# Holding back two heads' convolution chains, taking an output product two k-tiles at a time over both units, and two changes of order, in a two-layer mLSTM and attention trunk

## The chip, the cores and the metric

The program runs on one core of one Trainium2 chip. A core has engines that run side by side, each with its own queue of instructions taken in order: TensorE (PE: matmuls; its weight loads are shown apart as PEld), VectorE (DVE), ScalarE (ACT), GpSimd (POOL) and SyncE (SP, which here issues the loads from memory). They wait for each other through semaphores. PE writes to PSUM, eight banks of 128 x 512 numbers; everything else lies in SBUF. The metric is the device time of one execution in microseconds (us), lower is better.

## The reference

256 tokens of width 1024 pass through two layers. Each layer is a half-step SwiGLU (width 2752), a mixing block, a second half-step SwiGLU and a gated addition of a per-layer input ("ple"). The mixing block is where the change works:

```python
u = rmsnorm(h, mix_norm)
z = u @ w_in
...
m_qk = jax.nn.silu(causal_dwconv(m_qk, m_conv_w, m_conv_b))
...
hm = mlstm_chunkwise(mq, mk, mv, ig, lf)
hm = head_rmsnorm(hm, m_out_norm.reshape(M_HEADS, M_HEAD_DIM)).reshape(bsz, t, M_WIDTH)
hm = (jax.nn.sigmoid(m_o.astype(jnp.float32)) * hm).astype(h.dtype)
...
ha = swa_gqa_sinks(aq, ak, av, a_sinks)

merged = jax.nn.sigmoid(g_m) * (hm @ w_branch_m) + jax.nn.sigmoid(g_a) * (ha @ w_branch_a)
h = h + merged @ w_out
```

`mlstm_chunkwise` is a matrix memory with 4 heads of 256, its queries and keys passed through a causal convolution of 4 taps and SiLU; `swa_gqa_sinks` is attention over a window of 128 tokens with 16 query heads of 64 and 4 key heads. All is float32.

## The kernel before

**Products in three parts.** A float32 number x is split into a high part (x cast to the matmul's type) and a low part (x minus the high part). A product is three matmuls: high x high, high x low, low x high. Weights come from memory by SP's loads into two raw buffers, 1 MB each. ScalarE casts the high part (`wh`), VectorE subtracts to get the low part (`wl`), 128 x 1024 at a time, called a part (two k-tiles of 512 columns). A ring of eight parts holds them; a part's place is free again when PE has used it (`drop`, line 400). Activations are split in the same way: `uT` (normed input), `hmT` (memory's output), `haT` = `qT` (attention), `mT` (merged), each with a high and a low tile, both transposed (features on partitions).

**Stages of the mixing block**, in the order in which PE runs them: keys and queries (`kvq`), values (`v`), gate A (`gt`), the input and forget gates (`if`), the memory's queries and keys of heads 0 and 1 (`z`, two jobs: part 0 queries, part 1 keys), attention's output product (`ya`), output gate (`og`), `z` of heads 2 and 3, gate M (`gt`), the memory's output product (`ym`), and the product with `w_out` (`yo`). Between them stand short pieces: attention's scores (`sc`, lines 1361 to 1407), its output (`ha`), the memory's scores (`st`), decay matrices (`wt`), outputs (`num`) and transposes (`tp`).

**The order is a planner's.** For PE, ScalarE, VectorE and SP the order of instructions on the chip is that in which the program emits them. Work beside the matmuls is written as generators, called chains; each `yield` marks a point at which the chain waits for an engine. `Clock` (line 63) keeps a planned time for each engine; every emitted instruction is charged a cost:

```python
 68    COST = {"tensor": (0.0, 1 / 2400), "scalar": (0.12, 1 / 1120), "vector": (0.12, 1 / 960), "gpsimd": (0.3, 0.17)}
 69    SYNC = 0.1
```

that is, a fixed part and a part per element of a row, in us; `SYNC` is added before another engine may use the result. `now` is PE's planned time. `tick` (line 201) goes through the list `bg` of chains in the order in which they were started and advances each one whose planned due time has come; then `feed` (line 336) may start the split of one more weight part. It does so if a place in the ring is free, the load has arrived by plan, and neither ScalarE nor VectorE is planned to be busy for longer than a slack from now, 3 us, or 2 us with four or more unused parts in store (line 343). A chain that PE needs at once is carried to its end by `finish` (line 226), which lets the planned time pass. `start` adds a chain and advances it once; `defer` adds one that runs at the next tick.

**Loops that matter here.** `project_halves` (line 475) makes products with features on the PSUM partitions, 256 tokens as columns. `units` are halves of the output, 512 features each; each unit has four parts (k-tiles 0-1, 2-3, 4-5, 6-7). The first two parts of all units run first (`todo[0]`), then the last two parts of the first unit, then of the second (`todo[1]`). A tick stands ahead of every six matmuls of 256 columns. When a unit has had its last part, `use` is called for each of its two pairs of k-tiles. For `ym` this is `use_m` (line 982): VectorE multiplies with gate M and adds gate A's share (two operations on `mg`), ScalarE casts the high half of `mT`, VectorE makes its low half. `project` (line 411) makes `yo` with tokens on the partitions and 512 columns; for each part and block of 128 tokens it ticks, waits by plan for `mT` of that k-tile (`xT.wait`), and emits the three matmuls, in which the low half of `mT` is wanted in the third.

The memory's output for head 3 is k-tiles 6 and 7 of `hmT`, the last ones written. `conv` (line 1158) takes one PSUM bank of `z`: ScalarE starts the sum, VectorE adds three taps for each of two k-tiles (six operations on `cv`), ScalarE applies SiLU, and the result is split into `qk`. `head` then makes the memory's scores from the query and key parts.

`norm` (line 639) prepares the next block's input. Between the layers (`between`) its transposed halves are put off until the ple product has been made (`crossed`), and then `to_T` (line 521) transposes and splits at once.

Of the kernel before, what the change touches and what calls it, by code (L numbers as in the profile page):

```python
# [19 lines left out]
P = 128  # L20
# [14 lines left out]
RING = 8  # L35
STORE, HASTE = 4, 3
AHEAD = (3.0, 2.0)
ACTIVE = 5
LAG = 1.5
WARM = 5  # L40
# [126 lines left out]
class Trunk:  # L167
# [7 lines left out]
    def __init__(self, ctx, tc, a, out):  # L175
        self.tc, self.a, self.out = tc, a, out
        self.clock = Clock()
        self.nc = Core(self.clock, tc.nc)
        pool = lambda name, bufs, **k: ctx.enter_context(tc.tile_pool(name=name, bufs=bufs, **k))
        self.const = pool("const", 1)  # L180
        self.rawp = pool("raw", RAW)
        self.wp = pool("w", RING)
        self.slots = pool("slots", 22)
        self.gp = pool("g", 1)
        self.sc = pool("sc", 7)
        self.small = pool("small", 6)
        self.psum = pool("psum", 8, space=PSUM)
        self.dram = pool("dram", 1, space=bass.MemoryType.DRAM)
        self.n = 0
        self.jobs, self.bg, self.haste, self.second = [], [], False, None  # L190
        self.embedded, self.crossed, self.extra = {}, False, 0
        self.pending, self.loaded, self.store = deque(), deque(), 0
        self.free, self.raws = deque([0.0] * RING), deque([0.0] * RAW)
        self.consts()
# [5 lines left out]

    def tick(self):

        for chain in list(self.bg):
            if chain[1] <= self.clock.now:
                self.advance(chain)
        self.feed()

    def advance(self, chain):
        if chain not in self.bg:
# [3 lines left out]
            self.bg.remove(chain)  # L213
        chain[1] = self.clock.end(outer)

    def later(self, chain, ready=0.0):

        self.bg.append([chain, max(self.clock.done(), ready)])
        return self.bg[-1]

    def start(self, chain):
        chain = self.later(chain)
        self.advance(chain)
        return chain

    def finish(self, chain):
        while chain in self.bg:
            self.tick()
            ahead = [c[1] for c in self.bg if c[1] > self.clock.now]
            if ahead and chain in self.bg:  # L230
                self.clock.wait(min(ahead))

# [103 lines left out]
    def feed(self, must=False):  # L336

        clock = self.clock
        if not self.loaded or not self.free:
            return  # L340
        raw, parts = self.loaded[0]
        part, arrival = parts[0]
        slack = AHEAD[self.store >= STORE]
        if not must and max(self.free[0], arrival, clock.t["scalar"] - slack, clock.t["vector"] - slack) > clock.now:
            return
        if not must and (self.second is not None or self.haste and self.store >= HASTE + self.extra):
            return
        self.store += 1
        ready = max(self.free.popleft(), arrival)
        parts.popleft()  # L350
        last = not parts
        if last:
            self.loaded.popleft()
        w = part.k * part.n
        hi = self.wp.tile([P, QU], F32R, tag="wh", name=self.name("wh"))[:, :w]
        lo = self.wp.tile([P, QU], F32R, tag="wl", name=self.name("wl"))[:, :w]

        def chain():
            src = raw[:, part.c0 : part.c0 + w]
            if part.gain is not None:  # L360
                for j in range(part.k):
                    o = slice(j * part.n, (j + 1) * part.n)
                    self.nc.scalar.mul(hi[:, o], src[:, o], part.gain[:, j : j + 1])
                yield
                for j in range(part.k):
                    o = slice(j * part.n, (j + 1) * part.n)
                    self.nc.vector.scalar_tensor_tensor(lo[:, o], src[:, o], part.gain[:, j : j + 1],
                                                        hi[:, o].bitcast(F32), op0=ALU.mult, op1=ALU.subtract)
            elif part.rows is None:
                yield from self.splitting(hi, lo, src)  # L370
            else:
                self.tc.nc.gpsimd.memset(lo[part.rows.stop :].bitcast(F32), 0.0)
                self.nc.scalar.copy(hi, src)
                yield
                r = part.rows
                self.nc.vector.tensor_tensor(lo[r], src[r], hi[r].bitcast(F32), op=ALU.subtract)
            part.ready = clock.done()
            if last:
                self.raws.append(part.ready)
                self.prefetch()  # L380

        part.hi, part.lo = (x.rearrange("p (k n) -> p k n", k=part.k) for x in (hi, lo))
        part.chain = self.later(chain())
        outer = clock.begin(dma=ready)
        self.advance(part.chain)
        clock.end(outer)
        return part.chain

    def need(self, part):

# [81 lines left out]
        self.project_halves([unit], xT, base, lambda k, ps: out.append(ps))  # L472
        return out

    def project_halves(self, units, xT, base, use):


        m = units[0][0].n // P
        ps = [[self.bank(base)[:, : min(2, m - c) * T] for c in range(0, m, 2)] for _ in units]
        todo = [[] for _ in range(2)]  # L480
        for u, unit in enumerate(units):
            k0 = 0
            for part in unit:
                todo[k0 >= KT // 2].append((u, k0, part))
                k0 += part.k
        for u, k0, part in todo[0] + todo[1]:
            for kk in range(k0, k0 + part.k):
                for c in range(m):
                    if (kk * m + c) * 3 % 6 == 0:
                        self.tick()  # L490
                        xT.wait(kk, *range(NT))
                        self.need(part)
                    cc, o = slice(c * P, (c + 1) * P), ps[u][c // 2][:, c % 2 * T : (c % 2 + 1) * T]
                    kw = dict(skip_group_check=True)
                    mm = self.nc.tensor.matmul
                    mm(o, part.hi[:, kk - k0, cc], xT[0](kk), start=kk == 0 and c % 2 == 0, stop=False, **kw)
                    mm(o, part.hi[:, kk - k0, cc], xT[1](kk), start=False, stop=False, **kw)
                    mm(o, part.lo[:, kk - k0, cc], xT[0](kk), start=False, stop=kk == KT - 1, **kw)
            self.drop(part)
            if k0 + part.k == KT:  # L500
                for i in range(0, m, 2):
                    use(u * m + i, ps[u][i // 2])
# [136 lines left out]
    def norm(self, t, ss, g, xT, between):  # L639

        r = self.scale(ss)
        if between and t:
            self.clock.stage["late"] = self.clock.done() + LAG
        yield
        xn = [self.scaled(t, n, r, g) for n in range(2)]
        if between and t:
            self.clock.stage["late"] = self.clock.done() + LAG
        yield
        while between and not self.crossed:
            yield  # L650
        for n in range(2):
            self.to_T(xn[n], xT, n * 4, t)
        if t == 0:
            self.haste = False
# [243 lines left out]
    def mix(self, l, xT, sink):  # L898
# [35 lines left out]
                rec.og_done.add((t, n))  # L934
            self.project(units_o, xT, "og", use)

        def job_T(units, xT, base, use, before=None):

            def run():
                if before is not None:  # L940
                    before()
                self.project_halves(units, xT, base, lambda *x: self.defer(use, *x))
            self.jobs.append(run)

        def gate(c0):
# [42 lines left out]
                yield from self.splitting(mT[0](k, n=2), mT[1](k, n=2), mg.rearrange("p (k t) -> p k t", k=2))  # L988
            mT.written(self.start(chain()), k, 2, *range(NT))

        job_T(self.pair_halves(a["w_branch_m"][l], 0), rec.hmT, "ym", use_m)
        job(self.pair(a["w_out"][l], 0), mT, "yo", then, prepare, last=4)
        return lambda: (self.per_feature(l), rec.prepare(w_in), att.prepare())

# [55 lines left out]
class Mlstm:  # L1050
# [97 lines left out]
    def qk_job(self, w_in, part, hp):  # L1148
# [3 lines left out]

        def run():
            for i, ps in enumerate(self.tr.project_T(unit, self.xT, "z")):
                self.tr.start(self.conv(ps, part, 2 * hp + i, c0 // P + 2 * i))
        self.tr.jobs.append(run)

    def conv(self, ps, part, hd, f):
# [106 lines left out]
class Swa:  # L1265
# [95 lines left out]
    def scores(self, t, p, acc, chains):  # L1361


        tr, nc = self.tr, self.nc
        S = (t + 1) * P
        per = NB // S
# [6 lines left out]
        for j0 in range(0, 4, per):  # L1373
            js = slice(j0, j0 + per)
            ps = [tr.bank("sc").rearrange("p (j s) -> p j s", j=per) for _ in range(2)]
            for j in range(per):
                for x, y in ((0, 0), (0, 1), (1, 0)):
                    for g in range(2):
                        nc.tensor.matmul(ps[g][:, j, :], self.qT[x](4 * p + j0 + j, tok, p=rows[g]),
                                         self.kT[rows[g], y, p, :S], start=j + x + y == 0, stop=x == 1,  # L1380
                                         skip_group_check=True)
            yield
            if t:
                for g in range(2):
# [99 lines left out]
```

## Time and profile before

| | |
|---|---|
| time, median of 3 runs | 1360.07 us (1359.92 to 1360.2) |
| the profiled execution's own time | 1359.88 us |
| its span, first instruction to last | 1358.2 us |
| ScalarE casts `wh`, 128 x 1024 | 405, mean 1049 ns |
| VectorE subtractions `wl`, 128 x 1024 | 405, mean 1221 ns |
| moved by DMA | 245.91 MB, mean 181 GB/s |

The page of the profile gives each engine's busy time and its share of the span, the chain of work that ended last, and the costliest groups of instructions. Rows of the timeline read: start in us from the span's start, duration in us, engine, line, operation, output tile <- input tiles, shapes, and xN where N instructions in a row are merged; in brackets the idle time of the engine before it and what ended it. `L133` is the line of a helper through which all recorded instructions pass, so groups are told apart by their tiles. Rows of the chain read: start, duration, engine and tile, number of instructions. The end of a matmul is modelled, so starts are what to compare.

### The profile page before, as it was taken

How to read it: one execution, taken by the hardware profiler on the slowest of the kernel's cores; microseconds unless marked ns; L12 is line 12 of the kernel's file. 1: busy time of each engine (PE TensorE's matmuls, PEld its weight loads, DVE VectorE, ACT ScalarE, POOL GpSimd, SP SyncE). 2: the span in 40 equal slices, each digit the busy share in tenths (PEclk: the TensorE clock that was granted, in tenths of full speed). 3: DMA queues.
4: the chain of work that ended last, by engine and by line, in shares of the span. 5: the costliest groups of instructions: out<-in, count | busy, mean ns of one | idle time of the engine just before them, and what ended most of it. 6: DMA issues, size and time to landing. Idle time of an engine off the chain costs nothing.

```text
span 1358.2 us, 22024 instructions
## 1 busy us (share of the span) xinstructions
PE 1350.5 (99%) x8974; PEld 1223.5 (90%) x8974; DVE 903.0 (66%) x1411; ACT 751.0 (55%) x1241; POOL 53.4 (4%) x82
## 2 busy tenths in 40 slices
PE   9999999999999999999999999999999999999998
PEld 7999887899899899988889998878998998999887
DVE  6766567888887755454665554578888877554545
ACT  6655446887565444443555443468875654444433
POOL 1000003000000000000000000030000000000000
PEclk9999999999999999999999999999999999999999
DMA  7755745354654475565466556463546554755651
GB/s 239 226 187 158 248 146 195 117 156 124 219 202 163 153 234 185 172 223 182 169 217 216 173 193 200 136 203 107 160 120 221 199 174 143 244 188 171 235 192 54
DMA packets 126789, 245.91 MB, mean 181 GB/s; under 512 B 15160, under 2 KB 24288, under 8 KB 126688
## 3 DMA queue, kind: packets, MB, share of 16 engines
q1 hardware_dynamic: 126672, 244.50, 55.9%
q8 instruction: 70, 1.15, 0.3%
q14 instruction: 31, 0.25, 0.1%
q10 hardware_dynamic: 16, 0.00, 0.0%
HBM read 242.39 MB, written 2.10 MB: 180 GB/s over the span
## 4 chain that ended last, share of the span: by engine, by line
PE 97%; DVE 2%; ACT 0%; DMA 0%; issue 0%; SPq 0%; DVEq 0%; ACTq 0%
PE dn L133 18%; PE pg L133 18%; PE pu L133 14%; PE gu L133 7%; PE gt L133 7%; PE z L133 7%; PE kvq L133 5%; PE og L133 3%; PE yo L133 3%; PE ym L133 3%; PE v L133 3%; PE tp L133 3%; PE ya L133 2%; PE sc L133 1%; DVE cv L133 1%; PE ha L133 1%
## 5 line engine op out<-in xcount | busy, mean ns | idle before, releaser
L133 DVE TENSOR_TENSOR wl<-raw,wh 128x1024 fp32r<-128x1024 f32 (+1 forms) x405 | 487.9, 1221 | 272.3 <-ACT wh L133 270.0
L133 ACT CAST wh<-raw 128x1024 fp32r<-128x1024 f32 x405 | 415.2, 1049 | 329.5 <-DMA raw<-in_ffn_w_down_dram 71.2
L133 PE MATMUL dn<-wh,hid 128*128 128x512 f32 x688 | 218.1, 395 | 0.0
L133 PE MATMUL pg<-uT,wh 128*128 128x256 f32 x1088 | 195.0, 282 | 0.0
L133 PE MATMUL pu<-uT,wh 128*128 128x256 f32 x1088 | 193.9, 281 | 0.0
L133 PEld LDWEIGHTS pg<-uT,wh 128*128 128x128 f32 x1088 | 166.8, 188 | 0.4
L133 PEld LDWEIGHTS pu<-uT,wh 128*128 128x128 f32 x1088 | 166.4, 188 | 0.0
L133 PEld LDWEIGHTS dn<-wh,hid 128*128 128x128 f32 x688 | 129.2, 188 | 30.7
L133 PE MATMUL pg<-uT,wl 128*128 128x256 f32 x544 | 152.6, 280 | 0.0
L133 PE MATMUL pu<-uT,wl 128*128 128x256 f32 x544 | 152.5, 280 | 0.0
L133 PE MATMUL dn<-wl,hid 128*128 128x512 f32 x352 | 139.2, 395 | 0.0
L133 PEld LDWEIGHTS pu<-uT,wl 128*128 128x128 f32 x544 | 102.7, 189 | 0.0
L133 PEld LDWEIGHTS pg<-uT,wl 128*128 128x128 f32 x544 | 102.7, 189 | 0.0
L133 PE MATMUL gt<-uT,wh 128*128 128x256 f32 x512 | 92.8, 282 | 0.0
L133 PE MATMUL z<-uT,wh 128*128 128x256 f32 x512 | 92.6, 283 | 0.0
L133 PE MATMUL gu<-wh,uT 128*128 128x512 f32 x256 | 81.4, 399 | 0.0
L133 PEld LDWEIGHTS gt<-uT,wh 128*128 128x128 f32 x512 | 79.1, 188 | 1.5
L133 PEld LDWEIGHTS dn<-wl,hid 128*128 128x128 f32 x352 | 66.1, 188 | 15.2
L133 PEld LDWEIGHTS z<-uT,wh 128*128 128x128 f32 x512 | 78.8, 188 | 0.6
L133 ACT ACTIVATE wh<-raw,gcol 128x512 fp32r<-128x512 f32 (+1 forms) x104 | 59.0, 638 | 29.0 <-DMA raw<-in_ffn_w_gate_dram 16.2
L133 DVE SCALAR_TENSOR_TENSOR wl<-raw,gcol,wh 128x512 fp32r<-128x512 f32 (+1 forms) x104 | 62.4, 654 | 17.6 <-ACT wh L133 17.6
L133 PE MATMUL z<-uT,wl 128*128 128x256 f32 x256 | 72.0, 281 | 0.0
(223 smaller groups left out, 2177.8 us busy)
## 6 DMA issues: line engine op xcount, KB each, us to landing
raw<-in_w_in_dram SPq DMA_DIRECT2D x60, 1024.0 KB
raw<-in_ffn_w_up_dram SPq DMA_DIRECT2D x40, 1024.0 KB
raw<-in_ffn_w_down_dram SPq DMA_DIRECT2D x40, 1024.0 KB
raw<-in_ffn_w_gate_dram SPq DMA_DIRECT2D x38, 1024.0 KB
raw<-in_w_branch_a_dram SPq DMA_DIRECT2D x16, 512.0 KB
raw<-in_w_branch_m_dram SPq DMA_DIRECT2D x8, 1024.0 KB
raw<-in_w_out_dram SPq DMA_DIRECT2D x8, 1024.0 KB
raw<-in_ple_gate_w_dram SPq DMA_DIRECT2D x8, 1024.0 KB
```

Source lines behind the costliest of these rows:

```text
L133: return issue(*args, **kw)
```

## The change

Four edits, and the planner that carries them:

- **Calm chains.** Chains get a third field, `calm`. `tick` doesn't advance a calm chain while `backlog`, the longer of ScalarE's and VectorE's planned busy times from now, is over `CALM`, 2 us. The conv chains of heads 0 and 1 (`hp == 0`) are started calm. `start` still makes their first step at once. `finish` counts the time at which the backlog falls to `CALM` among those it may wait for.
- **Turns.** For `ym` alone, the last two parts of both units are taken in the order of their k-tiles: unit 0 k 4-5, unit 1 k 4-5, unit 0 k 6-7, unit 1 k 6-7, where it was unit 0 k 4-5, k 6-7, unit 1 k 4-5, k 6-7.
- **Settle.** `feed` keeps a list of the weight-split chains it starts; between the layers, before `norm` transposes and splits its halves, `settle` advances those of them that are still open by one step.
- **Score order.** In `scores`, the matmuls of a bank's heads with the high half of the query come first for all heads, then those with the low half; before, each head's three followed one another.

```diff
+CALM = 2.0
...
     def tick(self):
 
         for chain in list(self.bg):
-            if chain[1] <= self.clock.now:
+            if chain[1] <= self.clock.now and not (chain[2] and self.backlog() > CALM):
                 self.advance(chain)
         self.feed()
+
+    def backlog(self):
+        return max(self.clock.t["scalar"], self.clock.t["vector"]) - self.clock.now
...
-    def later(self, chain, ready=0.0):
-
-        self.bg.append([chain, max(self.clock.done(), ready)])
+    def later(self, chain, ready=0.0, calm=False):
+
+        self.bg.append([chain, max(self.clock.done(), ready), calm])
         return self.bg[-1]
 
-    def start(self, chain):
-        chain = self.later(chain)
+    def start(self, chain, calm=False):
+        chain = self.later(chain, calm=calm)
         self.advance(chain)
         return chain
 
     def finish(self, chain):
         while chain in self.bg:
             self.tick()
-            ahead = [c[1] for c in self.bg if c[1] > self.clock.now]
+            ahead = [c[1] for c in self.bg if c[1] > self.clock.now] + [self.clock.now + self.backlog() - CALM]
+            ahead = [x for x in ahead if x > self.clock.now]
             if ahead and chain in self.bg:
                 self.clock.wait(min(ahead))
...
         part.chain = self.later(chain())
+        self.feeds.append(part.chain)
...
+    def settle(self):
+
+        for chain in self.feeds:
+            self.advance(chain)
+        self.feeds = []
...
-    def project_halves(self, units, xT, base, use):
+    def project_halves(self, units, xT, base, use, turns=False):
...
+        if turns:
+            todo[1].sort(key=lambda item: item[1])
         for u, k0, part in todo[0] + todo[1]:
...
         while between and not self.crossed:
             yield
+        if between:
+            self.settle()
         for n in range(2):
             self.to_T(xn[n], xT, n * 4, t)
...
-        job_T(self.pair_halves(a["w_branch_m"][l], 0), rec.hmT, "ym", use_m)
+        job_T(self.pair_halves(a["w_branch_m"][l], 0), rec.hmT, "ym", use_m, turns=True)
...
-                self.tr.start(self.conv(ps, part, 2 * hp + i, c0 // P + 2 * i))
+                self.tr.start(self.conv(ps, part, 2 * hp + i, c0 // P + 2 * i), calm=hp == 0)
...
-            for j in range(per):
-                for x, y in ((0, 0), (0, 1), (1, 0)):
-                    for g in range(2):
-                        nc.tensor.matmul(ps[g][:, j, :], self.qT[x](4 * p + j0 + j, tok, p=rows[g]),
-                                         self.kT[rows[g], y, p, :S], start=j + x + y == 0, stop=x == 1,
-                                         skip_group_check=True)
+            for j, x, y in [(j, 0, y) for j in range(per) for y in range(2)] + [(j, 1, 0) for j in range(per)]:
+                for g in range(2):
+                    nc.tensor.matmul(ps[g][:, j, :], self.qT[x](4 * p + j0 + j, tok, p=rows[g]),
+                                     self.kT[rows[g], y, p, :S], start=j + x + y == 0, stop=x == 1,
+                                     skip_group_check=True)
```

More of the change, by code (lines that the diff above doesn't have):

```diff
@@ L189, in __init__ @@
         self.n = 0
-        self.jobs, self.bg, self.haste, self.second = [], [], False, None
+        self.jobs, self.bg, self.haste, self.second, self.feeds = [], [], False, None, []
         self.embedded, self.crossed, self.extra = {}, False, 0
@@ L935, in output_gate, with job_T @@
             self.project(units_o, xT, "og", use)
-        def job_T(units, xT, base, use, before=None):
+        def job_T(units, xT, base, use, before=None, turns=False):
             def run():
@@ L941, in run @@
                     before()
-                self.project_halves(units, xT, base, lambda *x: self.defer(use, *x))
+                self.project_halves(units, xT, base, lambda *x: self.defer(use, *x), turns)
             self.jobs.append(run)
```

## The prediction

> **What bounds the kernel now.** I read the page first, then the chain of waits, then what TensorE (PE) waited for.
>
> ```profile
> span 1358.2 us, 22024 instructions
> PE 1350.5 (99%) x8974; PEld 1223.5 (90%) x8974; DVE 903.0 (66%) x1411; ACT 751.0 (55%) x1241; POOL 53.4 (4%) x82
> ```
>
> ```profile
> 43.71 11.34 PE pu L133 x96
> 472.38 16.71 PE gu L133 x72
> ```
>
> PE is busy for 99% of the span. A busy PE can still be a slow one, so the chain's runs give the rate: 96 matmuls of 256 columns in 11.34 us are 0.118 us from start to start, 72 of 512 columns in 16.71 us are 0.232 us. The change removes no matmul, so only PE's waits can be won, and any new wait of PE is paid in full.
>
> ```profile
> PE ya L133 <- DVE wl L133: 0.8, 2, 0.4
> PE sc L133 <- DVE qT L133: 0.4, 2, 0.2
> PE gu L133 <- DVE wl L133: 0.4, 1, 0.4
> ```
>
> ```profile
>   DVE hmT L133: 0.5, 2
> ```
>
> The columns of the first fence (PE's waits) are total us, times, longest; the last row is from the view of the tile `ym`: us and times that its engine sat idle for `hmT`. The four waits belong to the four edits: `ya` to the calm conv chains, `sc` to the score order, `gu` to `settle`, `ym` to `turns`. All prices below are worked out for layer 0 and doubled, except `gu`, which occurs once.
>
> **Calm conv chains.** They add and remove no instruction.
>
> ```profile
> 328.86 0.40 PE L133 MATMUL ya<-qT,wh 128*128 128x256 f32 x2
> 329.68 0.39 PE L133 MATMUL ya<-qT,wl 128*128 128x256 f32 x1 [0.42 <-DVE wl L133]
> ```
>
> ```profile
> 324.89 2.94 ACT L133 CAST wh<-raw 128x1024 fp32r<-128x1024 f32 x3
> ```
>
> ```profile
> 325.03 2.93 DVE L133 SCALAR_TENSOR_TENSOR cv<-z,feat,cv 128x255 f32<-128x255 f32 x6
> ...
> 328.41 3.49 DVE L133 TENSOR_TENSOR wl<-raw,wh 128x1024 fp32r<-128x1024 f32 x3
> ```
>
> The `wl` matmul was due at 328.86 + 2 x 0.118 = 329.10 and starts at 329.68: 0.58 us late. Its cast was over about 0.98 us (a third of 2.94) after 324.89, but on VectorE (DVE) six conv taps, 2.93 us, stand ahead of it. They are of heads 0 and 1. Held back while the planned backlog is over 2 us, they let `wl` go about 2 us sooner, more than the 0.58 needed. The gain is 2 x 0.58 = 1.16 us at most and 0 at least; I take 1.16. An earlier `wl` also frees its raw buffer sooner, so the next load goes out earlier on the same queue, in the same order; nothing here waits for a load. Should the activations change places, ScalarE (55% busy) has room. Next in line are the two `wl` behind it, 1.16 us apart (3.49 / 3) where PE needs one per 24 matmuls, 2.83 us: not late. What is delayed is the score product of head 0:
>
> ```profile
> 337.03 1.29 DVE L133 TENSOR_TENSOR qk<-cy,qk 128x512 fp32r<-128x512 f32 x2
> ```
>
> ```profile
> 339.80 1.32 PE L133 MATMUL st<-qk,qk 128*128 128x256 f32 x10
> ```
>
> It has 1.48 us to spare, and PE has `ya` and `og` to run meanwhile. If that cover is gone the price is what the taps are late, up to 2.93 us a layer (second rival).
>
> **`settle`** puts a pending `wl` ahead of the transposed input's split.
>
> ```profile
> 694.67 0.63 PE L133 MATMUL gu<-wh,uT 128*128 128x512 f32 x2
> 695.67 0.50 PE L133 MATMUL gu<-wl,uT 128*128 128x512 f32 x1 [0.36 <-DVE wl L133]
> ```
>
> ```profile
> 693.20 1.29 DVE L133 TENSOR_TENSOR uT<-tp,uT 128x512 fp32r<-128x512 f32 x2 [2.37 <-ACT uT L133]
> ```
>
> ```profile
> 688.47 2.05 ACT L133 CAST wh<-raw 128x1024 fp32r<-128x1024 f32 x2
> ```
>
> The matmul was due at 694.67 + 0.464 = 695.13 and starts 0.54 us late. The cast ended at 690.52, and DVE sat idle for 2.37 us up to 693.20, so this 1.2 us split fits into idle time at no price. Gain 0.54 us (0 to 0.54). For the first block of tokens the same step puts a `wl` ahead of a split that was not late:
>
> ```profile
> 684.67 1.29 DVE L133 TENSOR_TENSOR uT<-tp,uT 128x512 fp32r<-128x512 f32 x2 [0.53 <-ACT uT L133]
> ```
>
> ```profile
> 687.05 0.40 PE L133 MATMUL gu<-wh,uT 128*128 128x512 f32 x1
> ```
>
> It ends at 685.96, with a `wl` of 1.2 us ahead at 687.2, and PE needs the low half at 687.05 + 0.46 = 687.5: no price, by 0.3 us.
>
> **Score order.** The high halves of all heads of a bank go first.
>
> ```profile
> 231.12 0.74 DVE L133 SCALAR_TENSOR_TENSOR qT<-tp,feat,qT 128x512 fp32r<-128x512 f32 x1
> ```
>
> ```profile
> 231.21 0.50 PE L133 MATMUL sc<-kT,qT 64*128 64x256 f32 x4
> 231.91 0.73 PE L133 MATMUL sc<-kT,qT 64*128 64x256 f32 x8 [0.20 <-DVE qT L133]
> ```
>
> The pair that needs the low half of `qT` starts at 231.91, when DVE has written it (231.12 + 0.74). Two heads' groups run side by side, a pair in about the 0.118 us of one matmul; two more pairs now stand ahead, so 0.23 us of the wait is filled. Count of weight loads and columns is the same. Gain 2 x 0.23 = 0.46 us (0 to 0.46).
>
> **`turns`.** The wait for the last head's `hmT`, 0.5 us in two times by the row above, goes: two other k-tiles, 24 matmuls or 2.83 us, now stand before it. But the first unit's output then ends 24 matmuls before `yo` instead of 48, and what turns it into `yo`'s input `mT` has to fit into half the time.
>
> ```profile
> 436.97 0.39 PE L133 MATMUL ym<-hmT,wh 128*128 128x256 f32 x2
> ...
> 442.57 0.39 PE L133 MATMUL yo<-wh,mT 128*128 128x512 f32 x1
> ...
> 443.04 0.63 PE L133 MATMUL yo<-wh,mT 128*128 128x512 f32 x2
> ```
>
> ```profile
> 437.02 0.68 DVE L133 SCALAR_TENSOR_TENSOR mg<-gate,ym 128x512 f32<-128x512 f32 x1
> ...
> 439.66 1.22 DVE L133 TENSOR_TENSOR wl<-raw,wh 128x1024 fp32r<-128x1024 f32 x1
> 440.80 0.68 DVE L133 TENSOR_TENSOR mT<-mg,mT 128x512 fp32r<-128x512 f32 x1
> 441.40 1.22 DVE L133 TENSOR_TENSOR wl<-raw,wh 128x1024 fp32r<-128x1024 f32 x1
> 442.54 0.68 DVE L133 TENSOR_TENSOR mT<-mg,mT 128x512 fp32r<-128x512 f32 x1
> 443.14 0.68 DVE L133 SCALAR_TENSOR_TENSOR mg<-gate,ym 128x512 f32<-128x512 f32 x1
> ```
>
> Before, the first unit ends at 436.97. DVE runs its four `mg` operations (2.64 us, 437.02 to 439.66), a `wl` (1.14 us to the next start), and the low half of `mT` for k-tiles 0 and 1, done at 441.48, 4.51 us after the unit's end. `yo` needs it in its third matmul, 0.47 us after its start (443.04 - 442.57), which is 6.07 us after the unit's end: 1.56 us to spare. Now the unit ends 2.80 us later against `yo`, and the spare time is -1.24 us even if DVE keeps this order.
>
> It doesn't keep it. The order is the planner's, and its own constants (line 68, `SYNC`, the tick every six matmuls) settle it; I use them for the order alone. From the tick after the unit's end, planned us: ticks at 0, 0.64, 1.28, 1.92, then `yo`'s first at 2.56. The four `mg` take 4 x (0.12 + 512/960) = 2.61; the first pair is due at 1.31 + 0.1 = 1.41, so ScalarE's copy is issued at 1.92 and ends at 1.92 + 0.12 + 512/1120 = 2.50, and the low split is due at 2.60. The freed slot's cast goes at 0.64, so its `wl` goes at 1.92. At 2.56 the low split is 0.04 short of due, while the second unit's outputs, finished just then, are due: their four `mg` are issued first. The same rules give before's order (`wl`, `mT`, `wl`, `mT`, then the second unit's `mg`), as the rows show.
>
> In rows: 0.05 (437.02 - 436.97) + 2.64 + 1.14 + 2.64 + 0.68 = 7.15 us after the unit's end, with 0.04 for the signal 7.19; PE is due at 2.80 + 0.47 = 3.27. PE waits 3.9 us in each layer. The ends of this unknown wait are 0.1 us (the split ahead of `wl` and of the second unit: 0.05 + 2.64 + 0.68 = 3.37) and 5.1 us (one more `wl`); I take the middle order, the planner's. The split for k-tiles 2 and 3 follows at once (0.68) and is needed 12 matmuls, 2.8 us, on: no second wait. Behind the waiting matmul stands all of `yo`, and DVE runs on, so nothing is caught up.
>
> **Sum**, against the profiled execution's own 1359.88 us (its span and 1.7 us around it): + 2 x 3.9 - 0.5 - 1.16 - 0.54 - 0.46 = +5.1, or 1365.0. The median of the runs shown, 1360.07, lies 0.19 above it, so I say **1365.2**.
>
> **Rivals.**
> First, not slower: the low split goes out ahead of the second unit's four `mg`. It hangs on 2.60 against 2.56 planned us; any 0.04 us in the plan (PE planned to wait a little between, or the tick one matmul later) decides it. Then PE waits 4.51 + 0.04 - 3.27 = 1.28 us a layer: 1360.07 + 2.6 - 2.7 = 1360.0. For it: the margin is tiny. Against: no other PE work is planned inside those 24 matmuls. 13%.
> Second, a held conv keeps its PSUM bank: two pairs of `z` banks and four of `ya` are all eight, and PE would wait for a held conv's six taps, up to 2.93 us in each layer, with the `ya` gain lost as well: up to 1365.2 + 5.9 + 1.2 = 1372.3, with half of the taps late 1369. For it: the backlog rule favours everything else over these taps. Against: PE waited for no bank before. 6%.
> Third, the clock falls in the new wait.
>
> ```profile
> 1.68 2.32 PE L568 MATMUL heat<-heat 128*128 128x512 bf16 x5 [1.68 <-DVE heat L563]
> ```
>
> ```profile
> 7.24 1.88 PE gu L133 x7
> ```
>
> ```profile
> L568 PE MATMUL heat<-heat 128*128 128x512 bf16 x7 | 3.3, 620 | 1.7 <-DVE heat L563 1.7
> ```
>
> After the idle start five matmuls of 512 columns took 2.32 us; less 0.62 for the last, four starts lie 0.425 us apart, 1.83 times the 0.232 of later. By 7.24 seven took 0.27 each, waits included. So a cold PE is slow for 2.3 to 5.6 us and loses 45% of it, 1.0 to 2.5 us, in each layer: 1367.2 to 1370.2. For it: 3.9 us is by far PE's longest wait. Against: no row shows that so short a wait cools it. 8%. The Trainium skill, "TensorE: Matmul & The Clock Gate", section "Part 1: The HAM clock gate", speaks against this change: an idle window of about 3.4 us, free-running, halves PE's clock. By that rule a wait of 3.9 us holds a whole window only in some phases, so my sum goes without it; no wait in this trace is long enough to show it.
> Fourth, the change wins what it says: no wait at `yo`, as DVE gets all of `mT` out in time: 1360.07 - 2.7 = 1357.4. It needs a split 1.3 us sooner than before's own order allows. 6%. Fifth, the calm chains change nothing at `ya`: 1366.4, 4%.
> My forecast has 63%.
>
> **Range and chances.** The forecast's own cases run from 1362.9 (no `wl` among the eight `mg`: - 2 x 1.14) to 1367.9 (none of the gains). With the fifth rival and the lower halves of the second and third that leaves out some 25 in 100, so the range reaches down to the first rival: 1360.0 to 1368.8. What stays out is the fourth and the upper halves of the second and third, 13 in 100. A measurement tells about 0.2%, 2.7 us, from no change. Slower: 63 + 6 + 8 + 4 = 81%; within: the first and half of the fourth, 16%; faster 3%.
>
> **What would show it.** PE's waits: one row `yo` <- DVE `mT` near 3.9 us, twice; DVE's timeline before it: eight `mg` in two fours with one `wl` between, then `mT`. Rows for `ya`, `gu`, `hmT` gone, `sc` halved; granted clock 1.00 over `yo`. An `mT` split ahead of the second four, with 1.3 us of waiting, would prove my order wrong.

## The result, and the profile after

| | before | after |
|---|---|---|
| time, median of 4 runs each | 1359.99 us (1359.86 to 1360.2) | 1367.96 us (1367.59 to 1369.32) |
| the profiled execution's own time | 1359.88 us | 1368.07 us |
| mean granted TensorE clock of the profiled execution | 1.0 | 0.997 |

The ratio is 1.0061 (95% interval 1.0049 to 1.0073): slower by 8.0 us, where 5.1 were forecast. The time lies inside the range, 2.8 us above the point. The granted clock is the share of TensorE's full clock that the chip let it have. From the page of after:

```profile
span 1366.3 us, 22044 instructions
PE 1352.5 (99%) x8974; PEld 1224.7 (90%) x8974; DVE 902.7 (66%) x1411; ACT 753.8 (55%) x1243; POOL 52.6 (4%) x82
```

The matmuls are as many as before, yet PE is busy 2.0 us longer: some of them ran slower, as the last view of this section shows. PE's waits in after (total us, times, longest):

```profile
PE yo L134 <- DVE mT L134: 6.5, 2, 3.3
...
PE gu L134 <- ACT wh L134: 0.6, 2, 0.4
PE gu L134 <- ACT uT L134: 0.5, 2, 0.2
PE num L134 <- DVE mp L134: 0.2, 1, 0.2
```

The rows for `ya`, `sc`, `hmT` and `gu` <- `wl` are gone. One large row has come, at the place forecast. DVE's timeline of after, in layer 0:

```profile
438.12 0.68 DVE L134 SCALAR_TENSOR_TENSOR mg<-gate,ym 128x512 f32<-128x512 f32 x1
...
440.16 0.69 DVE L134 TENSOR_TENSOR mg<-mg,gate 128x512 f32<-128x512 f32 x1
440.77 1.22 DVE L134 TENSOR_TENSOR wl<-raw,wh 128x1024 fp32r<-128x1024 f32 x1
441.90 0.68 DVE L134 SCALAR_TENSOR_TENSOR mg<-gate,ym 128x512 f32<-128x512 f32 x1
...
443.94 0.69 DVE L134 TENSOR_TENSOR mg<-mg,gate 128x512 f32<-128x512 f32 x1
444.55 1.89 DVE L134 TENSOR_TENSOR mT<-mg,mT 128x512 fp32r<-128x512 f32 x3
```

Four `mg`, a `wl`, the second unit's four `mg`, and only then the low half of `mT`. Meanwhile PE, in its own timeline of after:

```profile
441.59 0.40 PE L134 MATMUL yo<-wl,mT 128*128 128x512 f32 x1
445.29 0.72 PE L134 MATMUL yo<-wh,mT 128*128 128x512 f32 x2 [3.30 <-DVE mT L134]
```

The third matmul of `yo` was due 0.23 us after the second, at 441.82, and starts at 445.29: 3.47 us late. In layer 1 it is 3.36 us. That is not all. The view of windows, cut at four stretches of 3.41 us (length, busy us and instructions of PE, PEld, DVE, ACT, POOL, then the granted clock, DMA share and GB/s):

```profile
443.12:446.53 3.41, 1.24 (x5) 1.05 (x6) 3.38 (x7) 1.56 (x2) 0.00 (x0) 1.00 0.24 95
446.53:449.94 3.41, 3.41 (x9) 2.65 (x8) 1.05 (x1) 0.98 (x2) 0.00 (x0) 0.50 0.32 62
1125.78:1129.20 3.42, 0.22 (x2) 0.09 (x1) 3.35 (x7) 1.56 (x2) 0.00 (x0) 1.00 0.57 226
1129.20:1132.61 3.41, 3.41 (x8) 2.67 (x9) 2.20 (x3) 0.00 (x0) 0.00 (x0) 0.50 0.08 7
```

After each stop the clock is granted at 0.50 for one stretch of 3.41 us. Half the work of such a stretch, 1.7 us, is lost. So 6.8 us of standing still and some 3.4 us of a slow clock make 10.2 of the 10.8 us by which the two `yo` stages are longer (first matmul of `yo` to first of `gu`: 23.12 to 28.67 us in layer 0, 23.17 to 28.46 in layer 1). Most of the rest is `gu`'s first matmul, which now waits for the transposed input (0.5 us in two times, above). Against 10.8 stand some 2.7 us won elsewhere, and the span grew by 8.1.

### The profile page after: what moved, and what is told of

It is laid out like the page before. It is cut to its first block, busy times and chain, and to the rows that moved or that the text cites. A ratio compares the mean times of both kernels' runs of the same rounds, so it can differ in the third digit from the quotient of the medians.

```text
span 1366.3 us, 22044 instructions
## 1 busy us (share of the span) xinstructions
PE 1352.5 (99%) x8974; PEld 1224.7 (90%) x8974; DVE 902.7 (66%) x1411; ACT 753.8 (55%) x1243; POOL 52.6 (4%) x82
## 4 chain that ended last, share of the span: by engine, by line
PE 95%; DVE 2%; DMA 1%; ACT 1%; issue 0%; SPq 0%; ACTq 0%; DVEq 0%
PE dn L134 18%; PE pg L134 17%; PE pu L134 14%; PE gu L134 7%; PE z L134 7%; PE gt L134 5%; PE kvq L134 5%; PE yo L134 3%; PE v L134 3%; PE ya L134 3%; PE og L134 3%; PE tp L134 2%; PE ym L134 2%; PE sc L134 1%; DVE wl L134 1%; DMA raw<-in_w_branch_m_dram 1%
```

## The experiments

Two questions: does DVE's order at `yo`, and the clock behind it, carry the whole loss; and are the other three edits the gain they were priced at? The theory was the prediction's with the clock added; the rival, that part of the loss sits in the calm chains.

**1. Turns off (e1_no_turns).** Everything else of after stays.

```diff
-        job_T(self.pair_halves(a["w_branch_m"][l], 0), rec.hmT, "ym", use_m, turns=True)
+        job_T(self.pair_halves(a["w_branch_m"][l], 0), rec.hmT, "ym", use_m)
```

> The changed kernel with turns off and the three other edits kept. Theory (turns alone makes the wait at yo, and the wait alone makes the clock fall): no wait of PE for mT, granted clock 1.00 over both yo stages, and the gains of the three other edits stand: 1360.0 - 1.2 (ya) - 0.5 (gu between the layers) - 0.5 (sc) = 1357.8 us, or 0.9 more if the new waits of gu for uT right after yo come from the calm chains and not from turns. Rival (the calm chains, by holding banks or moving the plan, cost part of the 8 us): 1361 us or more.

Measured: 1363.19 us (1360.76 to 1365.9, 11 runs) beside 1360.15 for before; ratio 1.0024 (1.0015 to 1.0033). A miss: without the guilty edit the kernel is still slower than before. The `yo` wait is gone, and PE's waits show another:

```profile
PE ym L134 <- ACT hmT L134: 2.6, 2, 1.5
PE ym L134 <- DVE hmT L134: 1.9, 2, 0.9
```

Before, `ym` waited 0.5 us for `hmT`; now 4.5. So one of the three edits left makes the last head's output late, and turns, which puts 24 matmuls ahead of it, hides that in after. The wait of `gu` for `uT` isn't among this run's rows, and it is there in experiment 2 (0.5 us in two times), so it comes with turns. The runs lie in two groups, since the clock falls in some executions and not in others (mean granted clock 0.997 in those near 1365, 0.998 to 1.0 in the rest).

**2. Turns alone (e2_turns_only)**, on before:

```diff
+        if turns:
+            todo[1].sort(key=lambda item: item[1])
         for u, k0, part in todo[0] + todo[1]:
...
-        job_T(self.pair_halves(a["w_branch_m"][l], 0), rec.hmT, "ym", use_m)
+        job_T(self.pair_halves(a["w_branch_m"][l], 0), rec.hmT, "ym", use_m, turns=True)
```

> The kernel before with turns alone. Theory: the same DVE order (four mg, wl, four mg, then mT) and a wait of 3.3 us in each layer, with the clock at half for 3.4 us after each: 1360.0 + 2 x (3.4 + 1.6) - 0.5 = 1369.5 us, about 1.5 above the changed kernel. Rival (the wait needs the calm chains too): 1359.5 us and no wait at yo.

Measured: 1370.23 us (1368.98 to 1371.94, 4 runs); ratio 1.0076 (1.0062 to 1.009). PE's waits:

```profile
PE yo L133 <- DVE mT L133: 6.6, 2, 3.3
...
PE ya L133 <- DVE wl L133: 0.8, 2, 0.4
```

As expected: this one edit makes the whole wait at `yo`, and before's small waits are back beside it. The clock fell too (0.997 or 0.998 in all four runs).

**3. The second unit's pairs stand back (e3_units_apart).** After, but a pair of the second unit begins only when the first unit's pair of the same rank is through, so that the first low half of `mT` goes ahead of the second four `mg`.

```diff
+        pairs = []
...
         def use_m(k, ps):
             def chain():
+                while k >= 4 and pairs[k // 2 - 2] in self.bg:
+                    yield
...
-            mT.written(self.start(chain()), k, 2, *range(NT))
+            pairs.append(self.start(chain()))
+            mT.written(pairs[-1], k, 2, *range(NT))
```

> The changed kernel, where the second unit's pairs begin their mg only when the first unit's pair two places before has been split. Nothing else moves. Theory (what PE waits for is the queue on VectorE, four mg of the second unit long): the split for k-tiles 0 and 1 is done 2.6 us sooner, PE waits 0.7 to 1.3 us in each layer, too short for the clock to fall: 1368.0 - 2 x 2.4 - 2 x 1.6 = 1360.0 us, up to 1 us more a layer if a later pair is late in turn. Rival (the wait comes from something else than that queue, such as the cast or the load): the wait stays over 3 us and the time at 1368.

Measured: 1361.21 us (1360.28 to 1362.55, 10 runs); ratio 1.0009 (1.0 to 1.0018). DVE's timeline, then PE's waits:

```profile
441.82 0.68 DVE L134 TENSOR_TENSOR mT<-mg,mT 128x512 fp32r<-128x512 f32 x1
442.43 0.68 DVE L134 SCALAR_TENSOR_TENSOR mg<-gate,ym 128x512 f32<-128x512 f32 x1
```

```profile
PE yo L134 <- DVE mT L134: 1.2, 2, 0.7
PE gu L134 <- ACT wh L134: 1.1, 2, 0.9
```

The low half starts 2.7 us sooner than in after (444.55), and the wait at `yo` falls from 6.5 to 1.2 us, with the order on DVE as the only edit. The 1.2 us that are left are put down to the halved distance, since before's order is back at this place. The clock stays at 0.999 to 1.0 in all ten runs.

**4. The wait filled (e4_filled_wait).** After, with 12 matmuls into an unread PSUM bank ahead of `yo`'s third in each layer. They compute nothing that is used. Their time is that of the wait, so PE is as late as ever but not idle.

```diff
-                    self.mm3s(held, t == 0 and group[0] > 1)
+                    self.mm3s(held, t == 0 and group[0] > 1, base == "yo" and i == 0 and k == 0)
...
         for low in (low_first, not low_first):
+            if fill and low:
+                idle = self.bank("fill")
+                for _ in range(12):
+                    self.tc.nc.tensor.matmul(idle, items[0][1], items[0][3], start=True, stop=True)
```

> The changed kernel with 12 idle matmuls of 512 columns put ahead of yo's third matmul, into a bank that nothing reads: 2.8 us of PE work inside the 3.3 us wait. Theory (PE's own idleness lets the clock fall): yo's third matmul starts when it did, the clock stays at 1.00, and the time falls by the slow phases, 2 x 1.6: 1364.8 us. Rival (the clock falls for another reason, or the slow phase costs nothing): 1368.0 us, clock 0.997 as before. If the fillers came late, the time would rise by up to 2 x 2.8.

Measured: 1364.66 us (1364.45 to 1365.23, 5 runs), clock 0.999 to 1.0. It is 3.3 us under after's 1367.96 although 24 matmuls were added. PE's timeline, then the view of windows over the stretch that was slow in after:

```profile
445.62 0.74 PE L134 MATMUL yo<-wh,mT 128*128 128x512 f32 x2 [0.56 <-DVE mT L134]
```

```profile
447.00:448.00 1.00, 1.00 (x6) 0.82 (x5) 0.90 (x1) 0.00 (x0) 0.00 (x0) 1.00 0.00 0
448.00:449.00 1.00, 1.00 (x6) 0.77 (x6) 0.00 (x0) 0.70 (x1) 0.00 (x0) 1.00 0.06 10
```

`yo`'s third matmul starts 3.94 us after its first (441.68), as in after (3.93: 445.29 less 441.36), so PE gets on no sooner. The second cost is the clock, then; it follows from PE's idleness, and it is worth 3.3 us here.

**5. The wait half filled (e4b_half_filled)**, the same with `range(5)`, to find how long a stop it takes.

> The changed kernel with 5 idle matmuls ahead of yo's third, 1.2 us, so that 2.1 us of the wait stay idle. If only a stop of over 3 us lets the clock fall: 1364.7 us, as with 12 fillers. If what counts is PE's share of activity over a few us: the clock falls in some runs or in all, 1366 to 1368 us.

Measured: 1365.99 us (1364.62 to 1367.52, 4 runs). PE's timeline in the profiled execution, then the windows in layer 1 and at the end:

```profile
441.86 1.31 PE L482 MATMUL fill<-wh,mT 128*128 128x512 f32 x5
445.33 0.73 PE L134 MATMUL yo<-wh,mT 128*128 128x512 f32 x2 [2.17 <-DVE mT L134]
```

```profile
1123.72:1127.13 3.41, 1.75 (x9) 1.09 (x7) 3.34 (x6) 1.58 (x3) 0.00 (x0) 1.00 0.71 283
1362.66:1363.10 0.44, 0.00 (x0) 0.00 (x0) 0.00 (x0) 0.00 (x0) 0.00 (x0) 0.50 0.00 0
```

Two runs had a clock of 1.0 and took 1364.62 and 1364.91; two had 0.997 and took 1367.07 and 1367.52. The profiled execution is one of the first two (1364.91). So with stops of about 2 us in each layer the clock falls in some executions only. The first window is cut at a whole number (69) of stretches of 3.41 us ahead of 1362.66, where this execution's clock falls after PE's last matmul: PE busy for 1.75 us of it was enough to keep the clock.

**6. Calm alone (e5_calm_only)**: before with the calm chains, and none of the other three edits. As a diff on after:

```diff
-        if between:
-            self.settle()
...
-        job_T(self.pair_halves(a["w_branch_m"][l], 0), rec.hmT, "ym", use_m, turns=True)
+        job_T(self.pair_halves(a["w_branch_m"][l], 0), rec.hmT, "ym", use_m)
...
-            for j, x, y in [(j, 0, y) for j in range(per) for y in range(2)] + [(j, 1, 0) for j in range(per)]:
-                for g in range(2):
+            for j in range(per):
+                for x, y in ((0, 0), (0, 1), (1, 0)):
+                    for g in range(2):
...
```

> The kernel before with the calm conv chains alone. Theory (formed on e1_no_turns: the calm chains win at ya but make head 3's hmT late, since weight casts that wait for their load now stand ahead of its steps on ScalarE): ya without a wait, ym waiting 2.2 us a layer for hmT; span of a run at full clock 1360.0 - 2 x 0.9 + 2 x 2.4 = 1363 us with 2 us around the span counted, and up to 3.4 more in runs where the clock falls. Rival (settle or the score order makes hmT late): no more than the 0.26 us a layer of before at ym, 1358.2 us.

Measured: 1364.55 us (1363.83 to 1365.51, 5 runs); ratio 1.0033 (1.002 to 1.0046). The calm chains by themselves cost 4.5 us, so the lateness of `hmT` in experiment 1 is theirs. PE's waits at `ym` are those of experiment 1:

```profile
PE ym L134 <- ACT hmT L134: 2.7, 2, 1.6
PE ym L134 <- DVE hmT L134: 1.9, 2, 0.9
```

What is delayed is seen first at head 0's scores, on PE:

```profile
349.07 1.33 PE L134 MATMUL st<-qk,qk 128*128 128x256 f32 x10
```

They ran at 339.80 before: 9.3 us later, not 2.93 at most. The profiled execution also shows when the clock falls. `ym` has two stops in each layer, 1.12 and 0.94 us in layer 0, 1.57 and 0.94 us in layer 1. The windows are cut at whole stretches of 3.41 us counted from 1117.93, where the clock falls (435.26 is 682.67 us ahead of it):

```profile
431.85:435.26 3.41, 1.97 (x15) 1.53 (x14) 2.05 (x3) 1.69 (x3) 0.00 (x0) 1.00 0.51 123
435.26:438.67 3.41, 2.80 (x24) 2.80 (x24) 1.06 (x3) 0.00 (x0) 0.00 (x0) 1.00 0.48 184
1114.51:1117.93 3.42, 0.95 (x5) 0.76 (x6) 1.56 (x2) 1.32 (x2) 0.00 (x0) 1.00 0.72 245
1117.93:1121.34 3.41, 3.41 (x18) 3.41 (x17) 0.39 (x1) 0.00 (x0) 0.00 (x0) 0.50 0.18 67
```

In layer 0 the second stop lies across an edge, PE is busy for 1.97 and 2.80 us of the two stretches, and the clock holds. In layer 1 both stops lie in one stretch, PE is busy for 0.95 us of it, and the clock falls at its end.

**7. Settle and score order alone (e9_settle_score)**: after without turns and with `calm=False` at the conv chains.

> The changed kernel without turns and with no chain calm: settle and score order are left. Theory: the waits at ya (0.58 us a layer) and ym (0.26) stay as before, those of gu between the layers and half of sc go: 1360.1 - 0.5 - 0.5 = 1359.1 us, clock 1.00. Rival (these two also move something behind them): 1360 us or more.

Measured: 1358.69 us (1358.3 to 1359.06, 11 runs) beside 1360.02; ratio 0.999 (0.9982 to 0.9999). These two edits win about 1.3 us (0.1 to 2.4 by the interval), as priced together (0.54 + 0.46) and a little over; the row for `sc` is gone and not halved. Of before's waits those at `ya` and for `hmT` (0.5 us in two times, in the view of the tile `ym`) are left:

```profile
PE ya L134 <- DVE wl L134: 0.9, 2, 0.4
```

**8. The casts of `w_branch_m` later (e12_late_casts).** Why do calm chains make head 3 late at `ym`, some 80 us after the taps were held? ScalarE's timeline, first of before, then of experiment 1:

```profile
413.05 0.52 ACT L133 CAST mp<-ws 128x384 fp32r<-128x384 f32 x1
414.91 0.48 ACT L133 ACTIVATE hm<-num,den 128x256 f32<-128x256 f32 x1 [1.34 <-DVE den L133]
```

```profile
416.28 1.05 ACT L134 CAST wh<-raw 128x1024 fp32r<-128x1024 f32 x1 [2.48 <-DMA raw<-in_w_branch_m_dram]
...
419.14 0.48 ACT L134 ACTIVATE hm<-num,den 128x256 f32<-128x256 f32 x1
...
420.05 0.52 ACT L134 CAST mp<-ws 128x384 fp32r<-128x384 f32 x1
```

With calm chains a weight cast stands in ScalarE's queue ahead of head 2's `hm` and head 3's `mp`. Its load isn't there, so ScalarE stands idle for 2.48 us, and `hm` runs 4.2 us later than before, `mp` 7.0. VectorE had the `den` that `hm` needs by 416.1, so `hm` stood behind the casts for 3 us. Before has no row of ScalarE waiting for a load of `w_branch_m`. Experiment 1, and then after itself, have:

```profile
ACT wh L134 <- DMA raw<-in_w_branch_m_dram: 14.6, 4, 4.7
```

```profile
ACT wh L134 <- DMA raw<-in_w_branch_m_dram: 14.9, 4, 4.7
```

The rival is that the heads are late because their own chains were held, whatever ScalarE does. The edit, on experiment 1, lets these splits start only 4 us after the load's planned arrival:

```diff
-        if not must and max(self.free[0], arrival, clock.t["scalar"] - slack, clock.t["vector"] - slack) > clock.now:
+        if not must and max(self.free[0], arrival + part.late, clock.t["scalar"] - slack, clock.t["vector"] - slack) > clock.now:
...
+        units_m = self.pair_halves(a["w_branch_m"][l], 0)
+        for part in units_m[0] + units_m[1]:
+            part.late = 4.0
+        job_T(units_m, rec.hmT, "ym", use_m)
```

> The kernel after with turns off (as in e1_no_turns), and the splits of w_branch_m's parts may start only 4 us after the load's planned arrival. Question: why does ym wait 2.2 to 2.8 us a layer for hmT once the conv chains are calm? Theory A: ScalarE stands at a cast of w_branch_m whose load has not come (3.7 and 2.5 us idle in e1_no_turns), and head 2's hm and head 3's sl and mp are queued behind it; with the cast planned later they go first, hm of head 2 runs near 415 instead of 419.1, the waits of ym for hmT fall from 4.5 us in total to under 1, and the time is 1357.5 to 1358.5 (1363.2 less 4.5, and without the clock's falls). Theory B: the heads are late because their conv chains were held, whatever ScalarE does; the waits stay near 4.5 us and the time at 1362 to 1363.

Measured: 1359.87 us (1359.49 to 1362.06, 11 runs) beside 1359.9; ratio 1.0001 (0.9992 to 1.001). ScalarE's timeline, then PE's waits:

```profile
412.59 0.47 ACT L135 ACTIVATE hm<-num,den 128x256 f32<-128x256 f32 x1 [0.72 <-DVE den L135]
...
414.01 0.52 ACT L135 CAST mp<-ws 128x384 fp32r<-128x384 f32 x1 [0.17 <-DVE ws L135]
...
417.18 1.99 ACT L135 CAST wh<-raw 128x1024 fp32r<-128x1024 f32 x2
```

```profile
PE gu L135 <- ACT uT L135: 2.4, 2, 1.2
...
PE yo L135 <- DVE mT L135: 0.5, 2, 0.4
PE gu L135 <- ACT wh L135: 0.5, 2, 0.2
```

The cast goes behind, `hm` and `mp` run 6 us sooner, and `ym` doesn't wait for `hmT` at all: the place of the casts in ScalarE's queue is the cause, and holding the chains is not enough of one. (The edit moves the parts' subtractions on VectorE as well; that the queue in question is ScalarE's is read from the rows above.) The time missed its expectation by 1.4 us, with 2.9 us of new waiting at `gu` and 0.5 at `yo`; what brings these was not tried. Why the calm chains bring the planner to put the cast there was not tried apart.

**9. Only the keys' chains calm (e11_calm_keys)**, with settle and score order, without turns.

```diff
-                self.tr.start(self.conv(ps, part, 2 * hp + i, c0 // P + 2 * i), calm=hp == 0)
+                self.tr.start(self.conv(ps, part, 2 * hp + i, c0 // P + 2 * i), calm=hp == 0 and part == 1)
```

> Settle and score order, no turns, and only the key chains of heads 0 and 1 calm (part 1), which were the ones ahead of the late wl. Theory (the delay of the heads comes from holding the query chains too): the wait at ya goes (1.2 us), hmT is late by 0.3 to 1 us a layer instead of 2.3: 1359.1 - 1.2 + 0.4 = 1358.3 us. Rival (any held chain delays the heads as much): 1361 us or more.

Measured: **1356.46 us** (1356.13 to 1357.41, 8 runs) beside 1360.02; ratio 0.9975 (0.9965 to 0.9985). It is faster than both kernels, and 1.8 us under what was expected, in part because `hmT` isn't late at all; the rival, that any held chain delays the heads as much, is out. All that PE waits for behind its start:

```profile
PE gu L134 <- ACT wh L134: 0.4, 1, 0.4
```

The waits at `ya` and for `hmT` are both gone without turns. Two chains are held instead of four, and head 0's scores come sooner than before, not later:

```profile
335.23 1.31 PE L134 MATMUL st<-qk,qk 128*128 128x256 f32 x10
```

## Why the prediction was right, and where it was not

**Right: sign, place and cause.** The planner's order of DVE, worked out to 0.04 us in the plan, came out as written in both layers, and experiments 2 and 3 show that this order makes 5.3 of the 6.5 us of waiting; the other 1.2 come with the halved distance, which the prediction had too. That the order held was decided by 0.04 planned us, as the prediction says of itself. The first rival (the split ahead of the second four `mg`) and the fourth (all of it wins) are out.

**Mis-sized: the wait at `yo`.** 3.9 us forecast, 3.47 and 3.36 measured. The term "0.05 (437.02 - 436.97)" counted from the unit's last matmul. But the unit's first pair sits in its own bank, which was through six matmuls earlier, and DVE took it at once behind a `wl`: its first `mg` starts at 438.12, 3.24 us ahead of `yo` (441.36) instead of the 2.75 that the sum held (2.80 less 0.05). This is 1.0 us too much over two layers. In before the first `mg` came 0.05 us after the unit's end because a `wl` stood ahead of it there, too, until 437.02:

```profile
435.88 1.22 DVE L133 TENSOR_TENSOR wl<-raw,wh 128x1024 fp32r<-128x1024 f32 x1 [1.75 <-ACT wh L133]
```

**Wrong: "my sum goes without it", the third rival.** The clock did fall, in both layers of the profiled execution of after, and the mean clock of 0.996 or 0.997 says the same of its other three runs. It cost 3.3 us in all (experiment 4). It was given 8%, and its price, 1.0 to 2.5 us in each layer, held what was measured, about 1.7. The reason given, "no row shows that so short a wait cools it", was a gap in the trace and no evidence against. By the Trainium skill, "TensorE: Matmul & The Clock Gate", section "Part 1: The HAM clock gate", the gate looks at free-running windows of 3413 ns. The trace agrees with both: the slow stretches are 3.41 us long, and their starts, 446.53 and 1129.20, lie 682.67 us apart, 200.0 such windows. The reading in the prediction that a whole window must be idle didn't hold, if the window that decides is the one just ahead of the fall: in the window ahead of the first slow stretch PE was busy for 1.24 of 3.41 us.

**Right in sum, for after: the gains.** 2.7 us were forecast from `ya`, `gu`, `sc` and `hmT`, and 10.8 less the span's 8.1 leaves 2.7. The account closes: 7.8 - 2.7 = 5.1 was the forecast; 6.8 of waiting + 3.3 of clock + some 0.7 left over, most of it at `gu`'s start, - 2.7 makes 8.1. In part it was luck that the time came out inside the range: the forecast's own cases end at 1367.9, and the range went beyond them because it had let in the lower halves of the second and third rivals.

**Wrong: "nothing here waits for a load" and the price of a delayed head.** The calm chains' delay was bounded by the taps' 2.93 us with 1.48 to spare. Head 0's scores moved by 9 us, ScalarE came to stand at a cast whose load wasn't there, and head 3's output was late by 4.5 us over two layers, with the clock's falls on top in some executions. In after ScalarE stands there as long (14.9 us), but no wait of PE shows it, because turns puts 24 matmuls ahead of the late `hmT`. So the sum of the gains was right by luck, with a gain too large for calm alone (a loss of 4.5 us, experiment 6) and a use of turns too small (it was given 0.5 us, and hides 4.5). The second rival, a held bank, didn't come: no wait of PE for a bank shows.

## What to carry to other kernels

Before two streams of work are brought closer to their common consumer, write down the order in which the helping engine will take its queue there; the halved distance is paid in whole operations that happen to stand in front. An edit that holds work back has to be measured without the edits beside it: here one edit hid the other's loss, and taking out the edit that looked guilty gave back only 4.8 of 8.0 us. A wait of TensorE of about 2 us or more can bring a slow clock behind it and is to be priced with that: for the stops of 3.3 us here it was half as much again.

## What the runs showed that was not expected

- The clock's fall followed how much of a stretch of 3.41 us PE was idle, and so where the stretches began, and not the length of one stop. It fell after stretches in which PE was busy for 0.22 and 1.24 us (after) and 0.95 us (experiment 6, two stops with work between); it held after 1.75 us (experiment 5) and 1.97 us (experiment 6). Where between 1.24 and 1.75 us it turns was not measured. That stops of about 2 us brought the fall in two of four executions of experiment 5 would fit, if the stretches lie differently against the kernel from one execution to the next; the two that fell have no profile, so it was not seen.
- Work that computes nothing can pay: 24 added matmuls made a kernel 3.3 us faster (experiment 4).
